# Constants of the second layer traced one per matmul and without priority; first eight output rows loaded and split in the fourth product of the last head

## The chip, the cores and the metric

The kernel runs on one core of a Trainium2 chip. The metric is the device time of one execution in microseconds (us). A core has five engines with queues of their own: TensorE (PE; its weight loads are listed as PEld), VectorE (DVE), ScalarE (ACT), GpSimd (POOL) and SyncE (SP), which issues DMAs. Each executes its instructions in the order of the program; semaphores make one wait for another.

## The reference, cut to what matters

Two residual layers over a sequence of 512 tokens of width 2048: `x <- x + W_out(mixer(RMSNorm(x)) * silu(gate))`. The first layer's mixer is gated differential attention with 8 heads, the second's is an RWKV-7 scan.

```python
def diff_attention_mixer(h, cos, sin, w_in, q_gain, k_gain, ..., subln_w, w_out, lambda_init):
    q, k, v, gate = jnp.split(h @ w_in, 4, axis=-1)          # 8 heads, two 128-wide q and k each
    q = apply_rope(rms_norm(q, q_gain), cos, sin)
    k = apply_rope(rms_norm(k, k_gain), cos, sin)
    o = causal_diff_attention(q, k, v, lam)                   # softmax 1 - lam * softmax 2, times v
    o = rms_norm(o, subln_w) * (1.0 - lambda_init)
    return (o * silu(gate)) @ w_out

def rwkv7_mixer(h, ..., mu, w0, a0, k_k, k_a, r_k, gn_w, gn_b, ...):
    p = h @ w_in
    p = p + (token_shift(p) - p) * mu                         # per-channel constants
    ...
```

What matters here is that the second layer needs small per-channel constants (`mu`, `w0`, `a0`, `k_k`, `k_a`, `r_k`, `gn_w`, `gn_b`, some halved or subtracted from one), which depend on nothing computed, and that the output projection of the first layer needs the attention output of all heads as rows of 128 channels, split in two halves.

## The kernel before, in words

**Products.** All large matmuls are done in float32 as three matmuls of a rounded high half and the low half that is left (`mm3`, L116): high by high, high by low, low by high. A split of a weight tile or an activation row costs one cast on ACT and one subtraction on DVE: L615 and L616 for weights of the heads, L109 and L110 for other weights, `split_row` (L471 to L480: cast L475, subtraction L476) for rows of the attention output.

**A head.** `Seven.head` (L658) computes the four projections of one head with seven products instead of eight (a Strassen-like scheme over halves of tokens and channels). A product is eight weight rows by two token blocks by three matmuls, 48 matmuls on PE. For every head but the second of the layer the order is P7, P2, P1, P4, P6, P5, P3; the text below calls them by these names. The weights of P7, P1, P4 and P5 lie in the tile `T`. When a product has split a group of two rows of it, `grow` has GpSimd add the next block of weights onto them by an accumulating DMA (L588); P4's rows are those that P1 was computed from, with such an addition. P3's weights are loaded anew by SP into the pool `wraw` (L590). Left-hand sides: P1 and P2 read rows 0 to 7 of the normalised input (`hH`, `hL`), P5 and P3 rows 8 to 15, P7, P4 and P6 read the sums S4, S2 and S1, made once. P7 of the last head is the last reader of S4, whose four tiles have the tags "LT" and "SX" (three of them), and P1 is the last reader of input rows 0 to 7. Results are taken out of PSUM by copies (L640) and takes (L645). After P5, `queries` (L647) rotates queries and keys (`rope`, L298): four token blocks, each with a scratch tile `t2` of tag "p1", which has one buffer. After P3, `VG.convert` makes V and the gate.

**What sets the order.** The program is written out by a scheduler that gives each instruction a priority, its place in the trace, which `high_priority(offset)` moves forward: 2000 for splits, weight loads and rotations (AHEAD), 5000 for takes and for every step of a `Chain` (SCAN), 4000 for SOLVE. On each engine, and for a buffer that several tiles want, what is more urgent among the ready goes first; each queue then runs in the order so fixed. A `Chain` (L124) is a generator that `tick` (L168) steps between matmuls: each `yield n` lets n matmuls pass, and only the first chain of the list counts. PE instructions of a step are queued behind the matmul at which it is traced. The attention of head h-1 is such a chain during head h.

**The constants.** `rwkv_consts` (L1219) is a chain that starts in head 2 when the attention of head 1 has ended. It loads the parameters (L213, L1228), turns them on PE (L222, L1235), copies them out of PSUM (L224, L1237), and makes ten tiles by one `tensor_scalar` each from the copy `pb`, whose tile has the tag "p1", and four more by two copies each (L1253, L1254). The ten products and eight copies are one step.

**The start of the output projection.** After the last head, `layer0` (L998 to L1001) allocates `Tt`, in the buffer of `T`, makes a `Feed` (L483) over the rows of the attention output, which lie in DRAM as `yd`, and starts the last head's attention as a chain. A `Feed` loads rows (L495, on SP) and splits them; its constructor loads six and splits four, and later calls, from within the first block of the projection (`unit_tok`, L184), split up to the row wanted and load six further on. Fourteen rows come from `yd`; the last two stay on the core.

```python
        Tt = g.work.tile([P, KP, 512], F32, name="Tt", tag="T", bufs=1)
        feed = Feed(g, g.yd, KT - 2, lambda k: Tt[:, (0, 1, 2, 3, 6, 7)[k % 6]], 6)
        rows = feed.rows
```

Of the kernel before, what the change touches and what calls it, by code (L numbers as in the profile page):

```python
# [13 lines left out]
F32 = mybir.dt.float32  # L14
# [9 lines left out]
P = 128  # L24
D = 2048
T = 512
KT = D // P
NT = T // P
NH = 8
# [9 lines left out]
AHEAD, SCAN, SOLVE = 2000, 5000, 4000  # L39
# [41 lines left out]
class Halves:  # L81


    def __init__(self, parts, n):
        self.parts, self.n = parts, n
# [38 lines left out]
class Chain:  # L124

    def __init__(self, g, steps, delay=0, at=0):
        self.steps, self.wait, self.at = steps, delay, at
        g.chains.append(self)  # L130

    def step(self, g):
        with g.tc.high_priority(offset=SCAN):
            self.wait = next(self.steps, None)
        if g.state and g.later:
            with g.tc.issue_after(g.state.ins):
                g.later.pop(0)()
        g.state = None
        if self.wait is None:
            g.chains.remove(self)  # L140
# [69 lines left out]
def fetch_rows(g, pieces, queue, tag="junk", bufs=2):  # L210
    t = g.tmpc.tile([P, P], F32, name="prow", tag=tag, bufs=bufs)
    for r0, n, ap in pieces:
        queue.dma_start(out=t[r0 : r0 + n, :], in_=ap)  # L213
    return t
# [268 lines left out]
class Feed:  # L483

    def __init__(self, g, src, n, home, ring=8):
        self.g, self.src, self.n, self.home, self.ring, self.raw, self.rows = g, src, n, home, ring, [], []
        self.load(6)
        self.split(4)  # L490

    def load(self, upto):
        for k in range(len(self.raw), min(upto, self.n)):
# [32 lines left out]
KP = 8  # L526
GROUPS = ((0, 2), (2, 2), (4, 2), (6, 2))
LOW = {"BKT": 2, "VS": 2, "AR": 3, "BK": 1, "LT": 1, "SX": 3}
QH, VH = 0, 1


class Seven:
# [114 lines left out]
    def queries(self, q, last):  # L647
# [7 lines left out]
        self.turning = Chain(self.g, keys(self.g, q, qkT, 9), 1, self.g.ticks + (42 if last else 34))  # L655
        return qkT

    def head(self, h):  # L658

        g, A, B, U, W, T = self.g, self.A, self.B, self.U, self.W, self.T  # L660
        q, q01, q23, held = QK(g, 0), [], [], []

        def tile_of(k, n):
            return [T[:, k : k + n]]

        def grow(k0, half):
            def then(k, n, raws):
                self.fetch(T[:, k : k + n], k0 + k, half, h, True)
            return then

        def renew(k, n, raws):
            if h + 1 < NH:
                self.fetch(T[:, k : k + n], KP + k, QH, h + 1)

        def keep(k, n):
            if k + n < KP:
                held.append(self.raw(n, k, VH, h))
            else:
                q23.extend(q.more(2))
                held.append([x[:, None, :] for x in q23])  # L680
                for i, x in enumerate(held[-1]):
                    self.fetch(x, k + i, VH, h)
            return held[-1]

        def widen(k, n, raws):
            for i, x in enumerate(raws):
                self.fetch(x, k + i, QH, h, True)

        P1 = self.rows(0, 1), tile_of, grow(0, VH)
        P2 = self.rows(0, 0), keep, widen  # L690
        P3 = self.rows(KP, 0), lambda k, n: self.raw(n, KP + k, VH, h)
        P4 = self.form("S2"), tile_of, grow(KP, VH)
        P5 = self.rows(KP, 1), tile_of, renew
        P6 = self.form("S1"), lambda k, n: held[k // 2]
        P7 = self.form("S4"), tile_of, grow(0, QH)
        sub = ALU.subtract

        if h == 1:
            self.product(A, *P2)
            self.prime(1)  # L700
            self.product(B, *P7)
            self.copy(U, A)
            self.product(A, *P1)
            q01.extend(q.more(2))
            self.copy(q01, B)
            self.take(q01, q01, U, sub)
            self.product(B, *P4)
            self.copy(W, A)
            self.take(W, W, U)
            self.product(A, *P6)  # L710
            self.take(q01, q01, B, sub)
            self.take(W, W, B)
            A, B = B, A
        else:
            self.product(B, *P7)
            self.product(A, *P2, end=False)
            q01.extend(q.more(2))
            self.copy(q01, B)
            self.product(B, *P1)
            self.copy(U, A)  # L720
            self.product(A, *P4, first=False)
            self.copy(W, B)
            self.product(B, *P6)
            self.take(q01, q01, A, sub)
            self.take(W, W, A)
        self.product(A, *P5)
        self.take(q01, q01, B)
        self.take(q23, B, W, sub)
        q.t1s = q01 + q23
        qkT = self.queries(q, h == NH - 1)  # L730
        self.product(B, *P3)
        self.take(W, W, A)
        for c in [c for c in g.chains if c is not self.turning]:
            c.finish(g)
        vg = VG(g)
        self.take(U, U, B)
        with g.tc.high_priority(offset=AHEAD if h == NH - 1 else 0):
            for t, x in ((2, W[0]), (3, W[1]), (0, U[0]), (1, U[1])):
                vg.convert(g, t, x)
        self.A, self.B = B, A  # L740
        return qkT + (q.sq, vg)
# [147 lines left out]
def layer0(g, aps):  # L889
# [3 lines left out]
    with ExitStack() as cx:  # L893
# [10 lines left out]
        def load_first(k0, ks, queue=None):  # L904
            return load_w(g, g.first[k0 // 2][0], aps["da_w_in"][0, 0], k0, ks, queue)
# [10 lines left out]
        with tc.high_priority(offset=AHEAD):  # L916
            xs += [xp.tile([P, NT, 512], F32, name=f"x{cb}") for cb in range(4)]
            g.first += [(g.wraw.tile([P, 2, 512], F32, name="wraw", tag="wraw"), i == 0) for i in range(3)]
            at = lambda k, n: (xs[k // 4], slice(k * P, (k + n) * P), slice(k % 4 * P, (k % 4 + n) * P))
# [3 lines left out]
            first = load_first(0, slice(0, 1), nc.scalar)  # L923
# [53 lines left out]
    with ExitStack() as cx:  # L977
# [15 lines left out]
        for h in range(1, NH):  # L993
            Chain(g, attention(g, h - 1, *before, 36), 14 if h > 1 else 28)
            if h == 2:
                Chain(g, rwkv_consts(g, aps), 8)
            before = u.head(h)
        Tt = g.work.tile([P, KP, 512], F32, name="Tt", tag="T", bufs=1)  # L998
        feed = Feed(g, g.yd, KT - 2, lambda k: Tt[:, (0, 1, 2, 3, 6, 7)[k % 6]], 6)
        rows = feed.rows  # L1000
        ch = Chain(g, attention(g, NH - 1, *before, 20, rows, Tt[:, 4:6]), 8)  # L1001

        def all_rows(n, m):
# [215 lines left out]
def rwkv_consts(g, aps):  # L1219
    nc, c = g.nc, g.const  # L1220
    r16 = lambda ap: ap.rearrange("(j p) -> j p", p=P)
    rows = [aps["rw_w0"][0], aps["rw_a0"][0], aps["rw_k_k"][0], aps["rw_k_a"][0],
            aps["rw_r_k"][0].rearrange("h n -> (h n)"), aps["rw_gn_w"][0], aps["rw_gn_b"][0]]
    pbs = [(16 * i, 16, r16(r)) for i, r in enumerate(rows)]
    mus_ = [(0, 64, r16(aps["rw_mu"][0, 0 : 4 * D]))]
    tb, tm = [fetch_rows(g, x, nc.gpsimd, t, 1) for x, t in ((pbs, "al"), (mus_, "yT"))]
    t = g.tmpc.tile([2, RK], F32, name="mut", tag="p0", bufs=1)
    nc.gpsimd.dma_start(out=t[:], in_=aps["rw_mu"][0, 4 * D :].rearrange("(j p) -> j p", p=RK))  # L1228
    yield 24
    pb = load_rows(g, pbs, 112, t=tb, o=g.tmpc.tile([P, 112], F32, name="prmpb", tag="p1", bufs=1))  # L1230
    yield 8
    g.mu = load_rows(g, mus_, 64, t=tm)
    yield 8
    ps = g.ps.tile([P, 512], F32, name="pt", tag="pa", bufs=2)
    nc.tensor.transpose(ps[:RK, :2], t[:], g.ident[:2, :2])  # L1235
    g.mut = c.tile([RK, 2], F32, name="mut2")
    nc.vector.tensor_copy(g.mut[:], ps[:RK, :2])  # L1237
    g.omu = c.tile([P, 64], F32, name="omu")
    g.omut = c.tile([RK, 2], F32, name="omut")
    nc.vector.tensor_scalar(g.omu[:], g.mu[:], -1.0, 1.0, ALU.mult, ALU.add)  # L1240
    nc.vector.tensor_scalar(g.omut[:], g.mut[:], -1.0, 1.0, ALU.mult, ALU.add)
    g.prm = {}
    for nm, i, a, b in (("hw0", 0, 0.5, 0.0), ("ha0", 1, 0.5, 0.0), ("kk", 2, 1.0, 0.0), ("nkk", 2, -1.0, 0.0),
                        ("hkk", 2, 0.5, 0.0), ("hka", 3, 0.5, 0.0), ("omka", 3, -0.5, 1.0),
                        ("hrk", 4, 0.5, 0.0), ("hgw", 5, 0.5, 0.0), ("hgb", 6, 0.5, 0.0)):
        o = c.tile([P, 16], F32, name="prm_" + nm)
        nc.vector.tensor_scalar(o[:], pb[:, 16 * i : 16 * i + 16], a, b, ALU.mult, ALU.add)
        g.prm[nm] = o

    for nm, first, second in (("bk_s0", "hkk", "hka"), ("bk_b0", "hkk", "omka"),  # L1250
                              ("bk_s1", "hka", "hkk"), ("bk_b1", "omka", "hkk")):
        o = c.tile([P, 16], F32, name="prm_" + nm)
        nc.vector.tensor_copy(o[:C], g.prm[first][:C])  # L1253
        nc.vector.tensor_copy(o[C:], g.prm[second][C:])  # L1254
        g.prm[nm] = o
    yield 8
# [667 lines left out]
```

## Time and profile before

| | |
|---|---|
| median of 3 runs | 2072.57 us (2072.24 to 2073.51) |
| the profiled execution | 2072.94 us |
| its span, first to last instruction | 2070.9 us |
| mean granted TensorE clock | 0.998 |
| ACT, POOL busy | 1277.6, 418.2 us |
| HBM traffic | 269.70 MB, mean 130 GB/s |

A page and a trace of one execution are given. In the timeline a line has the start, the duration, the engine, the line of the source, the operation, output and inputs by tile name, shapes, the number of instructions merged in the line, and in brackets the idle time before it and what ended that. Durations of matmuls overlap, so the distance from start to start is what a matmul costs. A line of the waits has the engine and its instruction, what it waited for, the total, how often, and the longest. A line of the windows has the stretch, and for each engine its busy time and number of instructions, then the granted clock, the share of time that the DMA engines were busy, and GB/s.

### The profile page before, as it was taken

The page shows a single profiled execution, that of the slowest core. Times are in us where ns is not written, and L with a number is a line of the kernel's source. Part 1 is how long each engine was busy: PE and PEld are TensorE (multiplying, and loading weights), DVE is VectorE, ACT ScalarE, POOL GpSimd, SP SyncE. Part 2 cuts the span into 40 slices and gives each one's busy share as a digit, 9 for nine tenths or more (in the row PEclk, how much of TensorE's full clock was granted, in tenths as well). Part 3 has the DMA queues.
Part 4 walks back from the last instruction along what each step waited for, and adds up shares of the span by engine and source line. Part 5 has one row for each costly group of instructions (what it writes and reads, how often), then busy time and mean ns, then how long its engine had stood idle before and what let it go on. Part 6 is the DMA issues. An engine that isn't in the chain of part 4 may idle for free. (4 is left out here: it accounts for less than half of the span.)

```text
span 2070.9 us, 35253 instructions
## 1 busy us (share of the span) xinstructions
PE 2051.2 (99%) x11924; PEld 1690.9 (82%) x11924; DVE 1678.3 (81%) x4379; ACT 1277.6 (62%) x3043; POOL 418.2 (20%) x733
## 2 busy tenths in 40 slices
PE   9999999999999999999999999999999999999999
PEld 7888878888888878887778888888888888877887
DVE  5979788887978886586878888888888888887745
ACT  5667666776767754455666666666666666665433
POOL 0020211202011000101233222323332223232001
PEclk9999999999999999999999999999999999999999
DMA  6387867869678666752222222222222222244665
GB/s 202 114 170 185 162 161 168 181 172 175 175 160 184 163 217 201 168 120 94 74 75 80 79 70 84 79 80 80 80 80 79 70 84 79 80 130 154 217 164 121
DMA packets 100773, 269.70 MB, mean 130 GB/s; under 512 B 12432, under 2 KB 28960, under 8 KB 100592
## 3 DMA queue, kind: packets, MB, share of 16 engines
q1 hardware_dynamic: 62016, 173.21, 26.4%
q0 software_dynamic: 24144, 78.23, 20.7%
q10 hardware_dynamic: 14432, 16.01, 2.2%
q8 instruction: 94, 1.54, 0.3%
q14 instruction: 87, 0.71, 0.1%
HBM read 251.41 MB, written 15.99 MB: 129 GB/s over the span
## 5 line engine op out<-in xcount | busy, mean ns | idle before, releaser
L118 PE MATMUL pp<-hH,wh 128*128 128x512 f32 x1024 | 416.6, 407 | 0.0
L118 PE MATMUL pp<-hL,wh 128*128 128x512 f32 x1024 | 411.9, 402 | 0.0
L118 PE MATMUL pp<-hH,wl 128*128 128x512 f32 x1024 | 411.6, 402 | 0.0
L109 ACT CAST wh<-wraw 128x512 fp32r<-128x512 f32 (+1 forms) x412 | 254.3, 618 | 220.1 <-PE pp L118 125.5
L110 DVE TENSOR_TENSOR wl<-wraw,wh 128x512 fp32r<-128x512 f32 (+1 forms) x412 | 292.8, 712 | 82.9 <-ACT wh L109 77.3
L118 PE MATMUL pp<-wh,hH 128*128 128x512 f32 x820 | 325.7, 398 | 0.8 <-DVE G L382 0.4
L118 PE MATMUL pp<-wl,hH 128*128 128x512 f32 x820 | 322.8, 394 | 2.3 <-DVE wl L616 2.3
L118 PE MATMUL pp<-wh,hL 128*128 128x512 f32 x820 | 321.9, 393 | 3.1 <-DVE hL L476 3.1
L118 PEld LDWEIGHTS pp<-hH,wh 128*128 128x128 f32 x1024 | 192.8, 188 | 37.9 <-issue 2.1
L118 PEld LDWEIGHTS pp<-hH,wl 128*128 128x128 f32 x1024 | 193.1, 189 | 33.2
L118 PEld LDWEIGHTS pp<-hL,wh 128*128 128x128 f32 x1024 | 193.2, 189 | 31.4
L118 PE MATMUL pp<-wh,S 128*128 128x512 f32 x672 | 214.3, 394 | 0.0
L615 ACT CAST wh<-T 128x512 fp32r<-128x512 f32 x224 | 137.3, 620 | 95.7 <-PE pp L118 77.4
L118 PEld LDWEIGHTS pp<-wh,hL 128*128 128x128 f32 x820 | 155.2, 189 | 35.2 <-DVE hL L476 3.6
L118 PEld LDWEIGHTS pp<-wl,hH 128*128 128x128 f32 x820 | 154.8, 189 | 33.0 <-DVE wl L616 3.2
L118 PEld LDWEIGHTS pp<-wh,hH 128*128 128x128 f32 x820 | 154.4, 188 | 32.9 <-DVE u L645 0.8
L1623 POOL COPY SA<-VS 64x64 f32<-64x64 f32 x224 | 75.1, 335 | 517.2 <-DVE VS L1641 463.9
L616 DVE TENSOR_TENSOR wl<-T,wh 128x512 fp32r<-128x512 f32 x224 | 150.9, 689 | 25.2 <-ACT wh L615 24.6
L588 POOL DMA_DIRECT2D T<-in_da_w_in_dram x84 | 72.1, 858 | 391.5 <-DMA wraw<-in_da_w_in_dram 193.8
L1488 DVE SCALAR_TENSOR_TENSOR tmpl<-LT,n,Tm 128x60 f32<-128x60 f32 (+24 forms) x496 | 135.9, 274 | 13.4
L118 PEld LDWEIGHTS pp<-wh,S 128*128 128x128 f32 x672 | 124.7, 188 | 24.4
L118 PE MATMUL pp<-wl,S 128*128 128x512 f32 x336 | 132.1, 393 | 0.2
(377 smaller groups left out, 4020.9 us busy)
## 6 DMA issues: line engine op xcount, KB each, us to landing
wraw<-in_rw_w_in_dram SPq DMA_DIRECT2D x128, 512.0 KB, 3.6
T<-in_da_w_in_dram POOLq DMA_DIRECT2D x84, 512.0 KB, 6.7
wraw<-in_da_w_in_dram SPq DMA_DIRECT2D x64, 512.0 KB, 3.9
T<-in_da_w_in_dram SPq DMA_DIRECT2D x28, 512.0 KB, 4.1
wraw<-in_da_w_out_dram SPq DMA_DIRECT2D x26, 512.0 KB, 4.4
wraw<-in_rw_w_out_dram SPq DMA_DIRECT2D x26, 512.0 KB, 3.9
wraw<-in_da_w_in_dram POOLq DMA_DIRECT2D x21, 512.0 KB, 6.9
xq<-in_x_dram SPq DMA_DIRECT2D x16, 256.0 KB, 4.5
```

The source lines that it names most:

```text
L109: nc.scalar.copy(hi[:], raw[:, k : k + n])
L110: g.split = nc.vector.tensor_sub(lo[:], raw[:, k : k + n], hi[:].bitcast(F32)).ins
L118: m = nc.tensor.matmul(out, a, b, start=s, stop=e, skip_group_check=skip)
L588: self.g.nc.gpsimd.dma_start(out=raw, in_=src, accum_op=ALU.add)
L615: g.nc.scalar.copy(hi[:], raw[:, k])
L616: g.nc.vector.tensor_sub(lo[:], raw[:, k], hi[:].bitcast(F32))
L1488: st = nc.vector.scalar_tensor_tensor(tt, LT[:, i : i + 1, i + 1 :].to_broadcast([P, s, n]), n2[:, i : i + 1], Tm[:, 0:s, i : i + 1].to_br ...
L1623: nc.gpsimd.tensor_copy(p.SA[r_, c - 1, :], VS[r_, c, h, :])
```

## The change

1. `Chain` gets a parameter `rank` (5000 as before unless given), the priority of its steps. The chain of the constants gets rank 0, its place in the trace.
2. In `rwkv_consts` each of the ten products is followed by `yield 1`, so that they are traced one matmul apart. The eight copies stay in one step.
3. `Feed` takes the numbers of its first loads and splits as `first`. A new method `first_rows`, called in the last head before its fourth product P4, makes the feed with rows 0 to 7 in four tiles in the buffers of S4, loads all eight and splits none; later rows go to `Tt` as before.
4. After each group of two weight rows of P4 in the last head, the feed splits two rows, eight in all.

```diff
-    def __init__(self, g, steps, delay=0, at=0):
-        self.steps, self.wait, self.at = steps, delay, at
+    def __init__(self, g, steps, delay=0, at=0, rank=SCAN):
+        self.steps, self.wait, self.at, self.rank = steps, delay, at, rank
...
-        with g.tc.high_priority(offset=SCAN):
+        with g.tc.high_priority(offset=self.rank):
             self.wait = next(self.steps, None)
...
-    def __init__(self, g, src, n, home, ring=8):
+    def __init__(self, g, src, n, home, ring=8, first=(6, 4)):
...
-        self.load(6)
-        self.split(4)
+        self.load(first[0])
+        self.split(first[1])
...
+    def first_rows(self):
+
+        g = self.g
+        pairs = [g.low.tile([P, 2, T], F32, name="yr", tag=t, bufs=LOW[t]) for t in ("LT", "SX", "SX", "SX")]
+        g.feed = Feed(g, g.yd, KT - 2, lambda k: pairs[k // 2][:, k % 2] if k < KP else g.spare(k), 6, (KP, 0))
...
             self.copy(U, A)
+            if h == NH - 1:
+                self.first_rows()
+                P4 = P4[0], P4[1], lambda k, n, raws: [grow(KP, VH)(k, n, raws), g.feed.split(k + n)]
             self.product(A, *P4, first=False)
...
-                Chain(g, rwkv_consts(g, aps), 8)
+                Chain(g, rwkv_consts(g, aps), 8, rank=0)
...
-        feed = Feed(g, g.yd, KT - 2, lambda k: Tt[:, (0, 1, 2, 3, 6, 7)[k % 6]], 6)
-        rows = feed.rows
+        g.spare = lambda k: Tt[:, (0, 1, 2, 3, 6, 7)[k % 6]]
+        feed, rows = g.feed, g.feed.rows
...
         g.prm[nm] = o
+        yield 1
```

## The prediction

> **What bounds the kernel now.** I read the page first: the span and the busy shares.
>
> ```profile
> span 2070.9 us, 35253 instructions
> PE 2051.2 (99%) x11924; PEld 1690.9 (82%) x11924; DVE 1678.3 (81%) x4379; ACT 1277.6 (62%) x3043; POOL 418.2 (20%) x733
> ```
>
> TensorE is busy for all but 20 us of the span. Nothing in the change removes a matmul, so all it can win is time in which PE stands or runs slowly. The waits of PE over the whole span come next (total, times, longest):
>
> ```profile
> PE pp L118 <- DVE hL L476: 3.1, 1, 3.1
> PE pp L118 <- DVE wl L616: 2.3, 2, 1.9
> ```
>
> These are its two largest waits, each with one long member, and the change touches both places. The longest of the second lies in head 2, where the constants of the second layer are made. The first lies where the last head ends and the output projection begins. What each place really costs is more than the wait, so I measured both against an undisturbed copy of the same work.
>
> **Part 1, the constants in head 2.** Heads repeat, so one fixed instruction of a head marks its beat. I take the first take after P6 (L645), from the timeline of DVE:
>
> ```profile
> 170.90 0.68 DVE L645 TENSOR_TENSOR t<-t,pp 128x512 f32<-128x512 f32 x1
> ...
> 259.04 0.68 DVE L645 TENSOR_TENSOR t<-t,pp 128x512 f32<-128x512 f32 x1
> ...
> 353.47 0.68 DVE L645 TENSOR_TENSOR t<-t,pp 128x512 f32<-128x512 f32 x1
> ```
>
> From head 1 to head 2 it is 88.14 us, from head 2 to head 3 it is 94.43. The stretch with the constants is 6.3 us too long, although its wait is only 1.9. The timeline of PE shows a second piece:
>
> ```profile
> 276.32 0.79 PE L118 MATMUL pp<-wl,hH 128*128 128x512 f32 x1 [1.85 <-DVE wl L616]
> ...
> 277.34 0.63 PE L118 MATMUL pp<-wl,hH 128*128 128x512 f32 x1
> 277.77 0.63 PE L118 MATMUL pp<-wh,hL 128*128 128x512 f32 x1
> ...
> 282.07 0.39 PE L118 MATMUL pp<-wh,hL 128*128 128x512 f32 x1
> 282.30 0.39 PE L118 MATMUL pp<-wh,hH 128*128 128x512 f32 x1
> ```
>
> After the wait the matmuls start 0.43 us apart, and 0.23 apart again by 282.07. The slow ones, some eight at 0.2 too long, run until about 280. So a wait costs its own length and some 1.7 us of slow matmuls behind it. The Trainium skill, "TensorE: Matmul & The Clock Gate", says under "Why this matters for your kernels" that only idle gaps beyond about 3 us cost clock. By that rule this place would give back little beyond its wait; the trace disagrees (1.85 us idle, then a pitch of 0.43), so the rows decide.
>
> Why it comes to a wait is in the timeline of DVE:
>
> ```profile
> 268.22 0.69 DVE L616 TENSOR_TENSOR wl<-wraw,wh 128x512 fp32r<-128x512 f32 x1 [0.67 <-ACT wh L615]
> 269.48 0.28 DVE L224 COPY prmpb<-prp 128x112 f32<-128x112 f32 x1 [0.57 <-PE prp L222]
> ...
> 274.68 0.42 DVE L312 TENSOR_TENSOR t<-t,ropeS 128x256 f32<-128x256 f32 x1
> ...
> 275.59 0.68 DVE L616 TENSOR_TENSOR wl<-wraw,wh 128x512 fp32r<-128x512 f32 x1
> ...
> 357.06 0.42 DVE L312 TENSOR_TENSOR t<-t,ropeS 128x256 f32<-128x256 f32 x1
> ```
>
> DVE splits no weight between 268.22 and 275.59: the 23 small products and copies of the constants, at priority 5000, stand in front of the splits at 2000. And the rotation of the head (L312) starts 15.6 us after the take (274.68 after 259.04), in head 3 only 3.6 us (357.06 after 353.47). Its scratch tile and the constants' `pb` share the one buffer of tag "p1": `pb`, more urgent, has it first and keeps it until the last of its ten products. So four rotations are pushed into the weights of P3 and of the next head.
>
> With rank 0 the splits (2000) and rotations (2000, same tag) go before `pb`; the constants fall into holes of DVE, and ten of their steps are each traced one matmul apart, so no long run of them forms. Head 3 shows whether holes follow; its windows (PE, PEld, DVE, ACT, POOL busy, clock, DMA share):
>
> ```profile
> 365.40:377.40 12.00, 12.00 (x56) 9.69 (x55) 12.00 (x35) 9.13 (x23) 0.88 (x1) 1.00 0.64 189
> 377.40:389.40 12.00, 12.00 (x63) 9.96 (x62) 10.76 (x25) 8.04 (x17) 3.43 (x4) 1.00 0.98 186
> 389.40:401.40 12.00, 12.00 (x58) 9.96 (x57) 7.92 (x22) 8.37 (x21) 3.41 (x4) 1.00 0.91 161
> ```
>
> DVE is full for one window with PE at full speed, and then has 1.2 and 4.1 us free. The 23 operations are about 4 us by their durations (0.28 for the copy above, some 0.17 for most). They fit, later; the layer that needs them starts hundreds of us after. What stays is their three PE transposes and the change of shape around each, which I put at 0.8 us (an estimate: the set of four in part 2 is busy 0.60). Value: 6.3 - 0.8 = 5.5, of which I take 5.3. Bounds: 2.1 (only the wait goes) and 6.3.
>
> **Part 2, the start of the output projection.** PE there, then DVE:
>
> ```profile
> 728.39 0.40 PE L118 MATMUL pp<-wh,hH 128*128 128x512 f32 x1
> ...
> 729.55 0.40 PE L118 MATMUL pp<-wl,hH 128*128 128x512 f32 x1
> ...
> 734.16 0.80 PE L118 MATMUL pp<-wh,hL 128*128 128x512 f32 x1 [3.14 <-DVE hL L476]
> ...
> 737.18 0.39 PE L118 MATMUL pp<-wh,hH 128*128 128x512 f32 x1
> ...
> 738.11 0.60 PE L361 MATMUL pt<-ident,t 128*128 128x128 f32 x4
> ```
>
> ```profile
> 727.74 0.70 DVE L110 TENSOR_TENSOR wl<-wraw,wh 128x512 fp32r<-128x512 f32 x1
> ...
> 729.54 0.70 DVE L645 TENSOR_TENSOR u<-u,pp 128x512 f32<-128x512 f32 x1
> ...
> 730.87 0.70 DVE L110 TENSOR_TENSOR wl<-wraw,wh 128x512 fp32r<-128x512 f32 x1
> ...
> 732.20 1.31 DVE L110 TENSOR_TENSOR wl<-wraw,wh 128x512 fp32r<-128x512 f32 x2
> 733.40 2.51 DVE L476 TENSOR_TENSOR hL<-Tt,hH 128x512 fp32r<-128x512 f32 x4
> ```
>
> Between 729.55 and 737.18 PE starts eight matmuls and one set of four transposes. At 0.23 each, and for the set the 0.60 of the like set at 738.11, that is 2.4 us; the place loses 7.63 - 2.4 = 5.2. The low halves of the first four rows come last of everything queued on DVE, at 733.40, behind conversions, takes and weight splits.
>
> After the change these rows are split long before. Late next is the second weight split, 730.87 to 731.57. PE has the first weight row for four token blocks before it needs that: 12 matmuls from 728.39, the first of the projection, to about 731.1; the bank of the fourth block is free at 730.24 (the take at 729.54). So PE stands about 0.5 us if it goes row by row, and some 2 if it goes block by block. I leave 1.0 us and take 4.2. Bounds: 0 (DVE, as full as now, makes something else late) and 5.2.
>
> **Part 3, what is put into the last head.** Eight splits on ACT and DVE and eight loads on SP move to the fourth product, P4. DVE there, in the same columns:
>
> ```profile
> 667.00:678.00 11.00, 11.00 (x55) 9.32 (x54) 9.23 (x32) 6.69 (x16) 3.44 (x5) 1.00 0.99 173
> 678.00:690.00 12.00, 12.00 (x64) 9.99 (x62) 9.28 (x31) 8.11 (x19) 2.58 (x4) 1.00 0.91 164
> 690.00:702.00 12.00, 12.00 (x63) 10.16 (x62) 9.29 (x29) 5.90 (x15) 0.00 (x0) 1.00 0.69 185
> ```
>
> Four splits took 2.51, so eight take 5.0; DVE is free for 1.8 + 2.7 + 2.7 = 7.2 us here. They have no priority, so the weight splits pass them; each can hold one up by 0.63 us, and PE has up to four split rows in hand. ACT has more room (eight casts near 0.6 each). Cost on the path: none by this cover, 5 if it were gone.
>
> The loads are the doubtful part. The first three lines are from the list of DMAs of the stretch 640 to 730 (queue; KB and time to landing), the others from timelines:
>
> ```profile
> q1 hardware_dynamic: 2476, 6.67, 22.4%
> ...
> T<-in_da_w_in_dram POOLq DMA_DIRECT2D x12, 512.0 KB, 6.6
> ...
> Tt<-yd SPq DMA_DIRECT2D x6, 256.0 KB, 4.4
> ```
>
> ```profile
> 666.15 0.88 POOL L588 DMA_DIRECT2D T<-in_da_w_in_dram  x1 [2.44 <-DVE wl L616]
> ...
> 674.33 0.61 ACT L615 CAST wh<-T 128x512 fp32r<-128x512 f32 x1
> ...
> 678.70 0.39 PE L118 MATMUL pp<-wh,S 128*128 128x512 f32 x1
> ...
> 690.25 8.35 SPq L590 DMA_DIRECT2D wraw<-in_da_w_in_dram  x3
> ```
>
> SP's timeline shows no issue in P1 or P4 ahead of the three weights of P3 at 690.25, so eight more issues hold up nobody there. But the DMA share is 0.99 and 0.91. At the sync queue's rate here, 6.67 MB in 22.4% of 90 us, or 330 GB/s, the 2.1 MB take 6.4 us of all engines. The weight that P4 starts with is added by the issue at 666.15, lands about 672.8, and must be cast by about 677 to be split for 678.70. That is 4.2 us of spare time. If the loads run as soon as their tiles are free (P7 has read them two products before P4, at 88.14 / 7 = 12.6 us each, so near 653), the adds behind them are late by 5 to 6 us, less the few tenths of free share: a wait of 0 to 2 us, with the slow matmuls behind it up to 4. If they run at their place in the program, after 678, they meet adds with over 10 us to spare. I take 0.7. In the sentence of a page: the Trainium skill, "DMA: Bandwidth & Descriptors", under "Issuing engines are not separate DMA queues", says that transfers of all engines interleave on the same 16 DMA engines, which speaks against this move; no row before shows the two queues meeting.
>
> Behind the change the projection's own feed loads six rows in place of the ones loaded and split now, with no reuse of a buffer among them. That frees DVE and SP after 740, where PE waits for neither, so it is worth nothing.
>
> **Sum.** -5.3 - 4.2 + 0.7 = -8.8 on the profiled execution, 2072.94 to 2064.1 (its span of 2070.9 and 2.0 us around it, which stay). The median of the three runs is 0.37 below that execution, so 2072.57 to 2063.8 us.
>
> **Rivals.** B: only the constants' stall goes, because DVE is full with or without the four low halves and the start of the projection still waits. For it: DVE's rows there follow one another with hardly a gap; against: the 12 matmuls that cover 731.57. -5.3 + 0.7: about 2068.0.
> C: only the projection gains; the tile `pb` still gets its buffer before the rotations, whatever its rank, and the run of constants only moves. Against: at rank 0 it stands 2000 behind them. About -2.1 - 4.2 + 0.7: 2067.0, or up to 2069.1 if nothing goes there.
> D: the loads collide with the adds for P4 at their full 2.1 MB over the 164 GB/s of the window 678 to 690, 12.8 us: less the 4.2 to spare, a wait of 8.6, and 1.7 of slow matmuls. -9.5 + 10.3: 2073.4, no change. The page's rule of the shared engines is this rival's.
> E, the slower one: SP puts the eight loads behind the three weights of P3, which it holds until 690.25 to 698.6. The rows then land near 705 (698.6, eight issues, 4.4 to land) while their low halves stand on DVE at their place in P4, near 684. DVE is in order, so weight splits stop for some 21 us; PE has four rows, 5.4 us, in hand, stands 16 and runs slowly 1.7. -9.5 + 17.7 = +8.2: 2080.8. It decides at one point, whether the first of these loads is issued before or after 690.25; SP lying empty before that speaks against it.
> F: the splits are placed so late that the change does nothing at the projection and the constants only move: 2072, counted with D.
>
> **How the numbers follow.** A measurement of this kernel tells about 0.2% from no change, 4.1 us, so faster means below 2068.4. Chances: forecast 0.57, B 0.15, C 0.09, D with F 0.11, E 0.08. The forecast, nearly all of B and a part of C are faster by more than that: 0.75. The rest of B and C, and D: 0.17. E: 0.08. The range goes from 2061.1 (6.3 and 5.2 both whole, nothing lost) to 2070.0, which takes in B, C and the lesser collisions and leaves out most of D and E. The likeliest case alone has 2061.1 to 2066.5 (a projection that keeps up to half of its loss).
>
> **What would show it.** Head 2 to head 3 by the same take: about 89 us instead of 94.4; the first L312 of head 2 within 4 us of the take; the ten L1247 products behind it and spread out; no wait for wl L616 of over 0.5. At the projection no wait of PE for hL L476, the second weight split as the latest thing, at most 1 us lost. In P4: eight L476 between 670 and 705, loads from yd on SP before 690, and PE at full busy time from 667 to 702. Wrong would be a PE wait in P4 for wl from T (D), DVE standing for a load (E), or a stall near 729 that has another name (B).

## The result, and the profile after

| | before | after |
|---|---|---|
| median of 6 runs each | 2073.82 us | 2064.74 us (2063.69 to 2065.58) |
| the profiled execution, its span | 2072.94, 2070.9 us | 2065.58, 2063.5 us |
| mean granted TensorE clock | 0.998 | 1.0 |

The ratio is 0.9957, 95% interval 0.9944 to 0.9970: 9.1 us faster, where 8.8 was forecast. The two profiled executions, one of each kernel, are 7.4 us apart; the median before is now 2073.82, with three more runs than the prediction had (2072.57). The sum came out right; its terms less so, and most of what follows is about them.

The page of the kernel after, its span and busy shares:

```profile
span 2063.5 us, 35254 instructions
PE 2048.4 (99%) x11924; PEld 1689.0 (82%) x11924; DVE 1676.3 (81%) x4379; ACT 1276.0 (62%) x3043; POOL 417.8 (20%) x733
```

The same work is done; only idle and slow time of PE is gone. PE's waits over the whole span (what waited and for what, total, times, longest):

```profile
PE pt L423 <- ACT yT L450: 1.1, 1, 1.1
PE pp L118 <- DVE wl L616: 0.8, 2, 0.6
```

The wait for hL L476 (3.1) is no longer in the list, and the longest for wl L616 fell from 1.9 to 0.6 (at 131 us, outside the stretches of the change). The wait of 1.1 is new; it lies in head 2, at 323 to 324 us.

**Head 2.** The timeline of DVE after, the mark used in the prediction (the first take behind P6) in heads 1, 2 and 3:

```profile
171.68 0.68 DVE L645 TENSOR_TENSOR t<-t,pp 128x512 f32<-128x512 f32 x1
...
259.83 0.68 DVE L645 TENSOR_TENSOR t<-t,pp 128x512 f32<-128x512 f32 x1
...
270.27 0.27 DVE L224 COPY prmpb<-prp 128x112 f32<-128x112 f32 x1 [0.57 <-PE prp L222]
...
271.12 0.68 DVE L616 TENSOR_TENSOR wl<-wraw,wh 128x512 fp32r<-128x512 f32 x1
...
272.48 0.69 DVE L616 TENSOR_TENSOR wl<-wraw,wh 128x512 fp32r<-128x512 f32 x1
...
277.60 0.17 DVE L1256 TENSOR_SCALAR prm_hgb<-prmpb 128x16 f32<-128x16 f32 x1
...
277.83 0.41 DVE L312 TENSOR_TENSOR t<-t,ropeS 128x256 f32<-128x256 f32 x1
...
351.09 0.68 DVE L645 TENSOR_TENSOR t<-t,pp 128x512 f32<-128x512 f32 x1
```

Head 2 to head 3 takes 91.26 us instead of 94.43; about 89 was forecast. Weight splits now pass the constants (271.12, 272.48, and so on). But the first rotation (L312, 277.83) starts 18.0 us after the take, later than before, and right after the last constant has been read from `pb` (277.60). So the rotations did not get the buffer "p1" first, against the prediction, and the rule told above the prediction, that a buffer goes to the more urgent tile, did not hold for it.

**The projection.** PE after, then DVE after:

```profile
724.58 0.47 PE L118 MATMUL pp<-wh,hH 128*128 128x512 f32 x1
...
727.64 0.39 PE L118 MATMUL pp<-wl,hH 128*128 128x512 f32 x1
727.91 0.63 PE L361 MATMUL pt<-ident,t 128*128 128x128 f32 x4
728.30 0.47 PE L118 MATMUL pp<-wh,hL 128*128 128x512 f32 x1
```

```profile
724.35 0.68 DVE L110 TENSOR_TENSOR wl<-wraw,wh 128x512 fp32r<-128x512 f32 x1
...
725.28 0.68 DVE L110 TENSOR_TENSOR wl<-wraw,wh 128x512 fp32r<-128x512 f32 x1
725.88 1.28 DVE L645 TENSOR_TENSOR u<-u,pp 128x512 f32<-128x512 f32 x2
```

From 724.58 to 728.30 PE starts 14 matmuls and one set of four transposes in 3.72 us; at 0.23 and 0.60, as in the prediction, they need 3.8. Nothing is lost, where 5.2 was lost before. The second weight split, which was to be late next, ends at 726.0 and is ahead of the takes instead of behind them.

**The last head.** The end of P1, P4 (its first matmul is at 676.30) and P6 in the windows (PE, PEld, DVE, ACT, POOL busy, clock, DMA share, GB/s), then the list of DMAs of 640 to 730 us (KB, median time to landing), then SP:

```profile
667.00:678.00 11.00, 11.00 (x56) 9.26 (x55) 10.71 (x38) 9.59 (x24) 3.43 (x4) 1.00 1.04 184
678.00:690.00 12.00, 12.00 (x61) 9.99 (x60) 10.32 (x35) 7.77 (x18) 2.56 (x3) 1.00 0.98 186
690.00:702.00 12.00, 12.00 (x62) 10.11 (x61) 9.99 (x35) 5.89 (x12) 0.00 (x0) 1.00 0.57 172
```

```profile
T<-in_da_w_in_dram POOLq DMA_DIRECT2D x11, 512.0 KB, 6.5
yr<-yd SPq DMA_DIRECT2D x8, 256.0 KB, 11.5
...
wraw<-in_da_w_in_dram POOLq DMA_DIRECT2D x3, 512.0 KB, 9.3
```

```profile
641.38 10.63 SPq L495 DMA_DIRECT2D yr<-yd  x8
```

PE is full throughout, and DVE took the splits into free time (10.71 + 10.32 + 9.99 of 35, where it had 27.8). The eight splits (L476) start at 664.8 to 682.4, where 670 to 705 was forecast: two before these windows, and the first four within P1, although they are called in P4. The loads were issued from 641 to 652 us, as soon as P7 had read the tiles. They landed 6.8 to 16.4 us after their issue, 11.5 in the median, so all before P4 begins. The adds onto `T` have the median they had (6.5, 6.6 before), but most of them were issued after the rows had landed; the four issued beside the loads (638 to 653 us; before, 638 to 655) went from 7.2 to 9.0, and the three onto `wraw` from 6.9 to 9.3. By the same mark the last head takes 88.19 us, before it took 88.12.

The spans: -3.2 in head 2, -5.2 at the projection, +0.1 in the last head, and the execution after was 0.8 us late already at 171.68 (170.90 before): -7.5, against 2063.5 - 2070.9 = -7.4.

### The profile page after: what moved, and what is told of

It is laid out like the page before. It is cut to its first block, busy times and chain, and to the rows that moved or that the text cites. A ratio compares the mean times of both kernels' runs of the same rounds, so it can differ in the third digit from the quotient of the medians.

```text
span 2063.5 us, 35254 instructions
## 1 busy us (share of the span) xinstructions
PE 2048.4 (99%) x11924; PEld 1689.0 (82%) x11924; DVE 1676.3 (81%) x4379; ACT 1276.0 (62%) x3043; POOL 417.8 (20%) x733
## 5 line engine op out<-in xcount | busy, mean ns | idle before, releaser
L615 ACT CAST wh<-T 128x512 fp32r<-128x512 f32 x224 | 137.1, 621 | 94.2 <-PE pp L118 71.0
L616 DVE TENSOR_TENSOR wl<-T,wh 128x512 fp32r<-128x512 f32 x224 | 150.5, 686 | 25.4 <-ACT wh L615 24.8
```

The source lines that it names most:

```text
L615: g.nc.scalar.copy(hi[:], raw[:, k])
L616: g.nc.vector.tensor_sub(lo[:], raw[:, k], hi[:].bitcast(F32))
```

## The experiments

Theory at this point: two separate gains, weight splits that pass the constants (3.2) and low halves done before the projection (5.2), while the buffer "p1" still goes to the tile traced first. Rivals are named in each expectation. All ratios are to the kernel before on the same chip, with 95% intervals.

### One part at a time

`e1_constants` is the kernel before with only the rank and the steps of the constants:

```diff
-                Chain(g, rwkv_consts(g, aps), 8)
+                Chain(g, rwkv_consts(g, aps), 8, rank=0)
...
         g.prm[nm] = o
+        yield 1
```

> The constants' part alone, on the kernel before: rank 0 and one constant per step, the output rows as they were. Theory (the change's time is a sum of two separate parts; the constants' part is worth the 3.2 us by which head 2 to head 3 shortened, 94.43 to 91.26, because weight splits no longer stand behind the constants; the late rotations stay because the buffer of the constants' row still comes first): 3.2 us below before, ratio about 0.9985, head 2 to head 3 about 91.3 us, first rotation (L312) about 18 us after the take, and the projection still waits some 3 us for a row's low half. Rival (the step of the prediction on record: 5.3 us, the rest was lost elsewhere in that execution): 5.3 us below, ratio 0.9974, head 2 to 3 about 89 us, first rotation within 4 us.

Measured: 0.9983 (0.9974 to 0.9991), 2070.40 us. DVE of this kernel, the marks of heads 2 and 3:

```profile
258.84 0.68 DVE L645 TENSOR_TENSOR t<-t,pp 128x512 f32<-128x512 f32 x1
...
348.87 0.68 DVE L645 TENSOR_TENSOR t<-t,pp 128x512 f32<-128x512 f32 x1
```

That is 90.03 us, with the first rotation at 276.85, 18.0 after the take, and the wait for hL (3.1) still there at the projection. The trace gives this part 4.4 us, more than the 3.2 of the theory and less than the 5.3 of the prediction; the timed 3.5 lies between, with an interval that holds all three.

`e2_rows` is the other part: the changed kernel with the constants of the kernel before.

> The rows' part alone: eight rows loaded and split in the last head's fourth product, the constants as in the kernel before. Theory: the start of the output projection loses nothing any more, the fourth product loses nothing, so 5.2 us below before, ratio about 0.9975; head 2 to head 3 stays at 94.4 us. Rival (the prediction's 4.2 less 0.7): 3.5 us below, ratio 0.9983, with about 1 us left at the projection or in the fourth product. Rival (most of the change was the constants): less than 2 us.

Measured: 0.9976 (0.9967 to 0.9985), 2069.26 us; head 2 to head 3 94.45; no wait for hL at the projection; the last head 88.31. This is the theory. The parts add up within the noise: 3.5 + 5.0 = 8.5, against 9.1 together.

### Rank or steps

`e3_rank` has the rank 0 without the `yield 1`; `e4_steps` has the `yield 1` at the old rank.

> The kernel before with the constants' chain at rank 0, still traced in one step (no step per constant). Theory (the rank, not the cutting into steps, lets the weight splits pass the constants): head 2 to head 3 about 90 us, as with the whole constants' part alone (90.03 against 94.43 before), no weight split waits for a constant, ratio about 0.998. Rival (the cutting into steps does it: ten constants traced together still stand together on the DVE): 94.4 us, ratio 1.000.

> The kernel before with one constant per step, but at the old rank 5000. Theory (the rank does it): the constants are still taken ahead of the weight splits as soon as their row is there, so head 2 to head 3 stays at about 94.4 us and the ratio at 1.000. Rival (the steps do it): about 90 us and 0.998.

Measured: rank alone 0.9985 (0.9976 to 0.9994) and 90.59 us; steps alone 0.9999 (0.9990 to 1.0009) and 92.97. The rank is the whole effect that these runs can tell. Tracing one constant per matmul does nothing: at rank 5000 the ten still stand together on DVE (272 to 273 us in `e4_steps`), and PE waits as long as before. In the waits of PE of `e4_steps`, 255 to 360 us:

```profile
PE pp L118 <- DVE wl L616: 1.9, 1, 1.9
```

That its beat is 92.97 all the same, and not the 94.4 of its theory, has another reason, told at the end.

### The buffer

`e5_own_buffer` is the changed kernel with `pb` in a buffer that is idle there; `e6_own_buffer_before` is the kernel before with the same edit.

```diff
-    pb = load_rows(g, pbs, 112, t=tb, o=g.tmpc.tile([P, 112], F32, name="prmpb", tag="p1", bufs=1))
+    pb = load_rows(g, pbs, 112, t=tb, o=g.tmpc.tile([P, 112], F32, name="prmpb", tag="at", bufs=1))
```

> The changed kernel with the constants' row in a buffer of its own (tag at, which is idle there) instead of p1, the one that the rotations share. Theory (a buffer goes to the tile traced first, whatever its rank, so p1 is held until the last constant has been read): the first rotation comes within 4 us of the take instead of 18, the turning of the keys waits no longer, head 2 to head 3 falls from 91.3 to about 88.5, and the time is 2 to 3 us below the changed kernel (about 11.5 us below before, ratio 0.9945). Rival (the rotations are late because of the DVE's queue, or lateness costs nothing and the 3 us are transposes and weight waits): first rotation as late as before, or early with the same 91.3 us; no change against the changed kernel (ratio 0.9957).

> The kernel before with only the buffer of the constants' row changed: rank 5000 and all constants in one step stay. Theory (two separate losses of about 3 us each in head 2: splits behind the constants, and late rotations): the rotations come within 4 us, so about 3 us are gained (ratio 0.9986, head 2 to 3 about 91.5), while the constants still stand in front of splits. Rival (one loss, the late rotations pile work onto the DVE where the constants are): both go, 5 to 6 us gained, ratio 0.9973, head 2 to 3 about 89 us. Rival (the constants' rank alone matters): nothing gained.

DVE of `e5_own_buffer`:

```profile
260.67 0.68 DVE L645 TENSOR_TENSOR t<-t,pp 128x512 f32<-128x512 f32 x1
...
264.27 0.41 DVE L312 TENSOR_TENSOR t<-t,ropeS 128x256 f32<-128x256 f32 x1
...
271.11 0.28 DVE L224 COPY prmpb<-prp 128x112 f32<-128x112 f32 x1
```

The first rotation now starts 3.6 us after the take, as in an undisturbed head, and ahead of `pb`: that the buffer held it is shown. Head 2 to head 3 falls to 89.01 us, 0.9 above an undisturbed 88.13. The time, 2064.66 us, ratio 0.9956 (0.9942 to 0.9969), did not move against the changed kernel: 2 to 3 us had been expected. Part of that is that the late rotations cost less than I had read from the first trace: 90.03, 90.59, 90.37 and 90.48 in four kernels with late rotations and rank 0 (`e1_constants`, `e3_rank`, and the two of the next section), so 1.0 to 1.6 and not 2.3. In the kernel before the same edit gave 0.9983 (0.9974 to 0.9991) and 90.17 us, a gain of 4.3 in the trace, between the theory (about 3) and the first rival (5 to 6): the rotations pass, and the wait behind the constants shrinks to 1.0 without slow matmuls after it. The two causes feed one stall, so each alone gives back over 4 of the 5.4 us that both give (94.43 to 89.01); in each, some 1.5 are the slow matmuls behind the wait, of which the last section tells more.

`e10_after_again` and `e11_own_buffer_again` repeat the pair side by side.

> The changed kernel itself, run beside the next one on the same chip, to set a difference of about 1 us against the runs' own spread. Its first profiled execution had one wait of 1.08 us at 324 us (the transposes behind ScalarE, which had stood for a late weight add) that four runs with the same code there did not have. Theory: that wait was of this execution alone, so head 2 to head 3 is 90.0 to 90.6 us here, not 91.3; ratio 0.9957. Rival (the wait belongs to the change): 91.3 again.

> The changed kernel with the constants' row in its own buffer, once more, beside the changed kernel. Theory (the late rotations cost 1.0 to 1.4 us of PE and no more): head 2 to head 3 about 89.0, 1.0 to 1.5 us less than the changed kernel in the trace; in the timed runs 1 us or less, which their intervals of some 2.5 us cannot tell from nothing. Rival (the early rotations are paid back elsewhere): head 2 to 3 as before 89.0, but the heads after it longer by as much.

Measured: the changed kernel 0.9961 (0.9949 to 0.9974), 2065.33 us; with its own buffer 0.9952 (0.9938 to 0.9965), 2063.46 us and 88.98 in head 2. The difference has the expected size, and the intervals overlap. The heads after head 3 are not longer for it (88.14, 88.13, 88.11). The first expectation failed as a number: head 2 to head 3 of the changed kernel was 91.19, not 90.0 to 90.6. But the wait of 1.08 us at 324 was not there; another was, of 1.1 us at 273, where the transposes of `mu` waited for a load that GpSimd had issued 10.9 us after its last one (9.2 in the first execution). The excess over 90 is a late transfer or issue here or there, different in each execution; why it is late stays open.

### Load or split

`e7_late_trace` keeps the early loads but calls the splits after the last head; `e8_held_back` holds the first four also behind the last product.

```diff
-                P4 = P4[0], P4[1], lambda k, n, raws: [grow(KP, VH)(k, n, raws), g.feed.split(k + n)]
...
         feed, rows = g.feed, g.feed.rows
+        feed.split(4)
```

In `e8_held_back` the added line is `feed.split(4, g.m)`, where `g.m` is the last matmul so far.

> The changed kernel with the eight rows loaded as early, but the first four split by a call after the last head, as before (the other four by the projection's own calls): the splits are no longer put into the fourth product by hand. Theory (what counts is when the rows arrive: a split that is ready early is put into a hole of the DVE wherever it is written): the projection starts without a stall, and the time is that of the changed kernel, ratio 0.9957, the fourth to eighth low halves perhaps 0.5 us late. Rival (the place of the call in the fourth product does it): the wait of about 3 us for a low half is back, 5.3 us of the gain gone, ratio about 0.9982.

> The same as the run before it, but the first four splits are held behind the last product of the last head, so that the DVE's order is that of the kernel before while the loads stay early. Theory (the stall came from the low halves standing among the DVE's other work of that place, in front of the second weight split; not from the loads' landing): the wait of about 3.1 us for hL at the projection's first matmul comes back, with the slow matmuls behind it, and ratio is about 0.998. Rival (the rows' late landing made the stall): no stall although the splits come late, ratio 0.9957.

Measured: `e7_late_trace` 0.9961 (0.9946 to 0.9976), 2064.96 us; its first four L476 still stand at 664.55 to 670.56, in P1 (P4 begins at 676.08), and the others at 732 and after; PE does not wait for them. `e8_held_back` 0.9981 (0.9972 to 0.9991), 2069.89 us. Its waits of PE, 600 to 780 us:

```profile
PE pp L118 <- ACT hH L475: 3.5, 1, 3.5
```

The time is as expected, the wait is not quite: it is for the cast, not for the low half. The hold put the four casts behind the last product too (729.60 us), and in the kernel before they came early. There ScalarE has

```profile
720.81 0.61 ACT L475 CAST hH<-Tt 128x512 fp32r<-128x512 f32 x1
```

and the fourth cast ends at 724.08, while the low halves follow on DVE from 733.40 (in the prediction). The four rows had thus landed by 723.5 us at the latest, 10 us before the first low half. So the stall came from where the halves stand in the queues, not from the landing of the rows; and what moves them is the early load. Once a row is there, the scheduler puts its split into a hole, wherever it is written. The call inside P4 is not needed for the first four rows, and the other four need not be early.

### How near the loads are to a collision

`e9_double_loads` is the changed kernel with each of the eight rows loaded twice into its place.

```diff
+            for _ in range(2 if k < KP else 1):
                 self.g.nc.sync.dma_start(out=self.raw[k], in_=self.src[k * P : (k + 1) * P, :])
```

> The changed kernel with each of the eight rows loaded twice into the same place (4.2 MB instead of 2.1 MB beside the fourth product's weight adds; the second load of a row follows the first). Theory (the DMA engines have room: at 2.1 MB the adds still land in time): the rows land some 6 to 8 us later, the splits slip towards the next product, and PE waits 0 to 2 us in the last head; ratio 0.9957 to 0.9967. Rival (the collision of loads and adds is near its edge): PE waits over 4 us for weights in the fourth product, ratio 0.998 or more.

Measured: 1.0018 (1.0009 to 1.0027), 2077.88 us, 12.6 above the changed kernel beside it: the rival in size, though the long wait of PE is not for a weight. Waits from 655 to 700 us (behind L495 the lines of this kernel have numbers one higher: its L616 is the cast L615), then ScalarE's timeline, then a window:

```profile
ACT hH L475 <- DMA yr<-yd: 12.8, 4, 6.2
PEld pt L423 <- ACT yT L450: 10.2, 1, 10.2
PE pt L423 <- ACT yT L450: 9.9, 1, 9.9
```

```profile
680.02 0.61 ACT L616 CAST wh<-T 128x512 fp32r<-128x512 f32 x1
686.80 0.62 ACT L475 CAST hH<-yr 128x512 fp32r<-128x512 f32 x1 [6.16 <-DMA yr<-yd]
687.32 0.58 ACT L641 COPY u<-pp 128x512 f32<-128x512 f32 x1
687.80 0.63 ACT L450 ACTIVATE yT<-yt,subw 128x128 f32<-128x128 f32 x2
```

```profile
684.00:688.00 4.00, 0.00 (x0) 0.00 (x0) 0.55 (x1) 1.20 (x3) 0.00 (x0) 0.50 0.37 135
```

The cast of a row (L475) stands in ScalarE's queue among weight casts and attention. When its row is late, all of these stand behind it: four waits of 12.8 us together, and PE does nothing from 684 to 688. The second load of a row also has to follow the first, so its lateness is more than that of 2.1 MB more. With each row loaded once, ScalarE waits for a row in no trace of the last head. The changed kernel loses less, and by another wait. ScalarE and PE of `e10_after_again`, at the start of P4 (677.00):

```profile
674.97 0.62 ACT L475 CAST hH<-yr 128x512 fp32r<-128x512 f32 x1
676.02 0.62 ACT L615 CAST wh<-T 128x512 fp32r<-128x512 f32 x1 [0.43 <-DMA T<-in_da_w_in_dram]
676.54 0.62 ACT L475 CAST hH<-yr 128x512 fp32r<-128x512 f32 x1
```

```profile
678.22 0.55 PE L423 MATMUL pt<-ident,p 128*128 128x128 f32 x3 [0.83 <-ACT yT L450]
```

ScalarE stands 0.43 us for a weight add onto `T` (and 0.38 for the one before), and PE 0.83 behind the attention step that follows on ScalarE. There the last head took 89.14 us.

### Four rows and the own buffer

`e12_four_rows` is the changed kernel with `pb` in its own buffer, four rows loaded early, the others from `Tt` after the last head, and all splits called there.

```diff
-        pairs = [... for t in ("LT", "SX", "SX", "SX")]
-        g.feed = Feed(..., lambda k: pairs[k // 2][:, k % 2] if k < KP else g.spare(k), 6, (KP, 0))
+        pairs = [... for t in ("LT", "SX")]
+        g.feed = Feed(..., lambda k: pairs[k // 2][:, k % 2] if k < 4 else g.spare(k), 6, (4, 0))
...
+        feed.load(6)
+        feed.split(4)
```

> The constants' row in its own buffer, and only four of the output rows loaded into the freed forms (1 MB instead of 2.1 beside the weight adds); their splits and the loads of the other rows are called after the last head, as before. Theory (four rows cover the projection's start; the eight loads cost 0.2 to 1.0 us in the last head by making the weights late, and half of them cost nothing): head 2 to head 3 about 89.0, last head 88.1 to 88.2 us, no stall over 1 us at the projection; 0.5 to 1.5 us below the changed kernel, ratio about 0.9953. Rival (the other four rows come too late when they are loaded in the old place): a wait of 1 to 3 us for hL in the first 15 us of the projection, ratio 0.9960 or more. Rival (the loads' number does not matter in the last head): 88.4 to 88.8 as with eight.

Measured: 0.9946 (0.9932 to 0.9959), 2062.06 us (2061.11 to 2062.61). The marks of the last two heads, from DVE:

```profile
613.01 0.68 DVE L645 TENSOR_TENSOR t<-t,pp 128x512 f32<-128x512 f32 x1
...
701.16 0.68 DVE L645 TENSOR_TENSOR t<-t,pp 128x512 f32<-128x512 f32 x1
```

The last head takes 88.15 us, where the seven executions with eight early rows took 88.19 to 89.14; head 2 to head 3 takes 88.99, and the projection has no wait over 0.3. It is the fastest of the kernels. It is 11.2 us below the kernel before beside it, the changed kernel 9.1 and 8.8 in its two sets; its span is 2.9 below that of the changed kernel (2060.6 against 2063.5), 2.3 of that in head 2 (88.99 against 91.26). The intervals of the two ratios overlap, so that it beats the changed kernel is likely, not shown.

## Why the prediction came out right, and where its steps did not

**The stall behind the constants.** Right. The blocked weight splits were the cause, and priority the cure: with rank 0 PE has no wait for a weight left there, in the kernel after as in the experiments that have the rank.

**The rotations.** The step that failed is "with rank 0 the splits (2000) and rotations (2000, same tag) go before `pb`". The splits did, the rotations did not. `pb` is traced before `queries`, and it kept the buffer at rank 0 as at 5000 (first rotation 18.0 us after the take in `e1_constants`, 3.6 in `e5_own_buffer`). Rival C had this half; its other half, that the run of constants only moves, was wrong. Priority chose among instructions that were ready; the buffer went to the earlier tile in all kernels here. That this is the scheduler's rule I conclude from them; it was not tried with the order of tracing alone.

**The term of head 2, -5.3.** Mis-sized: -3.2 in the profiled execution and -4.4 where only this part was changed. What the buffer still costs is 1.0 to 1.6. The 0.8 left for the three transposes was right: 0.9 remains with the own buffer.

**The slow matmuls behind the wait, 1.7.** The prediction took them as sure to follow this wait; `e4_steps` has the same wait without them, and its beat is 1.5 us shorter. The prediction had set its trace against the rule that gaps beyond about 3 us cost clock ("TensorE: Matmul & The Clock Gate", "Why this matters for your kernels", in the Trainium skill). The measurement decides: waits of 1.85 and 1.87 us had slow matmuls behind them in the kernel before and in `e2_rows`, one of 1.87 had none in `e4_steps`, and one of 3.1 or 3.5 had them in all six kernels with such a wait at the projection. The last section shows what decided. Here it had little effect on the sum: the timed runs of the kernel before, with mean clocks of 0.997 to 0.999, probably hold both kinds.

**The term of the projection, -4.2.** Mis-sized: -5.2. The 1.0 kept for the second weight split was for something that moved: with the low halves gone from that part of the queue, the split was placed before the takes (725.28 and not behind them). The 5.2 is the loss of one execution; the last section has it larger in others.

**The term of the last head, +0.7.** Right in size: 0.1 in the profiled execution, 0.2 to 1.0 in six other executions with the eight loads, 0.4 on average of all seven (88.55 against 88.13). DVE took the splits as worked out, and the loads were issued far ahead of the weights of P3, so rival E had no case. Where a wait shows, it is of D's kind, an add that lands too late: ScalarE stood 0.3 to 1.3 us for adds onto `T` in `e5_own_buffer`, `e7_late_trace`, `e10_after_again` and `e11_own_buffer_again`, and for a row in none of the seven. But the loads do not share P4's time, as D had it; they have landed before it. `e8_held_back` splits no row in the last head and took 88.47, so the loads alone can cost this; by which way stays open. With the loads doubled the cost is nearer to E's, on another engine: ScalarE stands for a row. The prediction gave ScalarE half a sentence ("has more room"); room is not the matter where the queue is in order.

**The sum.** -8.8 forecast; -9.1 and -8.8 in two sets of timed runs. That it agrees so well is luck in part: the miss of 1 to 2 us in head 2 was made up by 1 at the projection and a few tenths in the last head, and nothing in the prediction made these cancel. One of its sums does not come out: with half of the projection's loss kept, the likeliest case ends at 2065.4 (-5.3 - 2.6 + 0.7), not 2066.5.

## What to carry to other kernels

Early loading is what let the split move; where its call was written did not matter for the first rows, so first ask which buffer keeps a load late. A priority moved instructions past each other, but a tile that shares a one-buffer tag with urgent work kept its turn: give it another buffer. A transfer that lands late stops more than its reader: the instructions queued behind the first one that reads it wait too (ScalarE's 12.8 us in `e9_double_loads`). So look at who stands behind that instruction, and load no more rows early than the start needs.

## What the hardware showed that was not expected

The same wait had two sequels. PE had stood 1.85 us in the kernel before and 1.87 in `e4_steps`, on the same instructions; behind it the granted clock fell to 0.50 in the one and stayed at 1.00 in the other, and the beats were 94.43 and 92.97.

The granted clock shows what decided. Within an execution it changes only at points that lie whole multiples of 3.4134 us apart: in the kernel before at 276.20, 279.62, 733.59 and 737.00 (from the first to the third 457.39, 134 times 3.4134). Here are windows from point to point (PE, PEld, DVE, ACT, POOL busy, granted clock, DMA share, GB/s), first the kernel before, then `e4_steps`, whose points are counted back from its fall at 734.17:

```profile
272.79:276.20 3.41, 1.68 (x7) 0.79 (x5) 3.32 (x18) 1.72 (x4) 0.00 (x0) 1.00 0.02 6
276.20:279.62 3.42, 3.30 (x8) 2.62 (x9) 3.42 (x10) 1.14 (x3) 0.00 (x0) 0.50 0.25 49
279.62:283.03 3.41, 3.41 (x19) 2.82 (x18) 2.89 (x5) 1.32 (x3) 0.00 (x0) 1.00 0.75 252
```

```profile
273.37:276.79 3.42, 2.73 (x11) 1.66 (x11) 3.22 (x21) 2.29 (x6) 0.00 (x0) 1.00 0.12 48
276.79:280.20 3.41, 2.23 (x10) 1.79 (x11) 3.41 (x11) 1.17 (x3) 0.00 (x0) 1.00 0.00 0
280.20:283.61 3.41, 3.41 (x18) 2.82 (x17) 3.41 (x8) 1.92 (x5) 0.00 (x0) 1.00 0.71 201
```

In the kernel before nearly the whole wait lies between two points, and PE is idle for 1.73 of 3.41 us there. In `e4_steps` a point cuts the wait in two, 0.68 and 1.19 idle, and the clock stays. In `e2_rows` all 1.87 us lie between two points (275.89 and 279.30); the clock falls, and the beat is 94.45. Over all fourteen traces, from 25 to 1980 us, PE was idle for 1.66 to 2.86 us in the stretch before each of the nine falls, and for at most 1.60 in every other stretch that began and ended at full clock. This is read from the traces, with ends of matmuls that the profile models; no run moved the points on purpose.

The length of a fall varies too. At the projection it lasted one stretch in the kernel before and in `e4_steps`, and two in `e1_constants`, `e3_rank`, `e6_own_buffer_before` and `e8_held_back`:

```profile
724.39:727.80 3.41, 1.70 (x7) 0.74 (x5) 3.41 (x9) 2.53 (x6) 0.00 (x0) 1.00 0.53 189
727.80:731.21 3.41, 1.63 (x6) 1.45 (x7) 3.41 (x6) 0.00 (x0) 0.00 (x0) 0.50 0.73 197
731.21:734.62 3.41, 3.41 (x10) 2.53 (x9) 1.41 (x3) 1.10 (x2) 0.00 (x0) 0.50 0.86 288
```

These are of `e1_constants`. From the mark of the last head to the L446 at 775.82 us (in the kernel before) it takes 69.8 and 69.9 us with one stretch, 70.7 to 71.2 with two, and 64.5 to 64.6 without the wait. So a wait of 3.1 us (3.5 in `e8_held_back`) costs 5.3 us or some 6.4, by how long the clock stays low behind it.

The eight loads of 256 KB landed in 11.5 us in the median while accumulating adds ran beside them, and 256 KB loads of the same rows in 4.4 us at the projection before. The adds onto `T` beside them went from 7.2 to 9.0, those onto `wraw` from 6.9 to 9.3. So of the two, the plain loads lost more.
